# Left-side tiles moved by 192 bytes, and tokens' high and low part moved in one 512-column product over stationary weights

## Chip, core and metric

The kernel runs on one core of one Trainium2 chip. The metric is the device time of one execution in microseconds (us), the median of several runs. TensorE multiplies, VectorE and ScalarE move and transform tiles between SBUF and PSUM, GpSimd does a few small operations, and SyncE issues the DMAs that load weights.

## What is computed

A trunk of four post-norm layers over 256 tokens of width 1024. Each layer has a token mixer (layers 0 and 3 a gated linear recurrence, layer 1 an RWKV-7 time mix, layer 2 chunked attention), a cross-attention of 4 heads into 256 memory tokens, and an MLP with a squared ReLU. Cut to what matters:

```python
def memory_cross_attention(x, mem, w_q, w_kv, w_o):
    q = (x @ w_q).reshape(bsz, seq, MEM_HEADS, MEM_HEAD_DIM)
    kv = (mem @ w_kv).reshape(bsz, mem.shape[1], 2, MEM_HEADS, MEM_HEAD_DIM)
    s = jnp.einsum('bqhd,bkhd->bhqk', q, kv[:, :, 0]) * (MEM_HEAD_DIM ** -0.5)
    p = jax.nn.softmax(s, axis=-1)
    o = jnp.einsum('bhqk,bkhd->bqhd', p, kv[:, :, 1]).reshape(bsz, seq, d)
    return o @ w_o

def squared_relu_mlp(x, w1, w2):
    return jnp.square(jax.nn.relu(x @ w1)) @ w2

for i in range(DEPTH):
    y = mixer(i)(h)
    h = _layer_norm(DEEPNORM_ALPHA * h + y, ln_g[i, 0], ln_b[i, 0])
    y = memory_cross_attention(h, mem, mx_w_q[i], mx_w_kv[i], mx_w_o[i])
    h = _layer_norm(DEEPNORM_ALPHA * h + y, ln_g[i, 1], ln_b[i, 1])
    y = squared_relu_mlp(h, mlp_w1[i], mlp_w2[i])
    h = _layer_norm(DEEPNORM_ALPHA * h + y, ln_g[i, 2], ln_b[i, 2])
```

All inputs and weights are float32.

## The kernel before

**Three products for one.** Large matrix products are made in the type float32r from split operands. A float32 tile is split into a high part (ScalarE casts it to float32r, L436 and L338) and a low part (VectorE subtracts the high part, L437 and L339), and a product of two split operands is the sum of high × high, high × low and low × high. Each of the three is one matrix multiplication with a weight load of its own (the stationary operand) in front. Such three are called a trio below.

**Weights.** They come in chunks of 128 rows by 1024 columns (896 for the recurrence's input). A chunk is fetched by a DMA on SyncE's queue into wraw (four buffers) and split into whi and wlo (seven buffers each). A chunk is given back (`done`) when its last product is issued, and then the next chunk's split and DMA are issued; ScalarE and VectorE run their instructions in the order in which the code writes them.

**Two ways round.** `gemm` (and `mm_piece`, L272 to L274) has the tokens stationary, 128 by 128, and moves 512 (or 448) columns of weights. `gemm_t` has the weights stationary and moves the tokens, so that the result comes out transposed: four chunks, two halves m, in each half two output blocks g, and for every chunk two row blocks k; at each such place three products of 256 columns (L297, in `wt_steps`): whi × hthi, whi × htlo, wlo × hthi. The 256 columns are two runs of 128 tokens. `gemm_t` is used by the MLP's w1 for seven of its eight blocks (two banks of mm for m = 0, two of tp for m = 1; the first of the seven uses four banks of acc), for the second half of the cross-attention's q, and for three of the attention's six projections. It gives back the left 256 columns of each PSUM bank; the eviction is ScalarE's Relu (L709), a scaled copy (L960), or a cast and VectorE's subtraction (L610, L611). The memory pieces (`mem_piece`) run either `wt_steps` on the memory's tokens memhi and memlo, or trios of 512 columns with them stationary (L498).

**The MLP's loop.** For each block of 512 hidden columns: w1 of this block, then w2 of the block before (trios of 512 columns with ahi, alo stationary, 48 products). One round is 96 products of `gemm_t` and 48 of w2.

**Where tiles lie.** Pools are stacks in each partition's memory: the constants, LayerNorm's weights, the tokens (hthi, htlo) and every stage's own pool grow from the left, the weights (wraw, whi, wlo) and the memory's tiles from the right. The constant mhalf is 16 floats (64 bytes) and is the second tile of the left.

Of the kernel before, what the change touches and what calls it, by code (L numbers as in the profile page):

```python
# [7 lines left out]
F32 = mybir.dt.float32  # L8
F32R = mybir.dt.float32r
AF = mybir.ActivationFunctionType  # L10
ALU = mybir.AluOpType
# [5 lines left out]
T = 256  # L17
# [185 lines left out]
class _LazyT:  # L203
# [11 lines left out]

    def both(self, kt):

        return [x[:, :, kt, :] for x in self.hl]

    def __getitem__(self, t):  # L220
        if self.t[t] is None:
# [10 lines left out]
class Kern:  # L232
# [45 lines left out]
                self.st.done(c)  # L278

    def wt_piece(self, accs, chunks, both, m, last=False):  # L280
        for _ in self.wt_steps(accs, chunks, both, m, last):
            pass

    def wt_steps(self, accs, chunks, both, m, last=False):

# [28 lines left out]
    def gemm_t(self, name, idx, x, banks):  # L314

        ch = self.chunks(name, idx, 4, 128, 1024)
        for m in range(2):
            accs = [banks[m](), banks[m]()]
            self.wt_piece(accs, ch, x.both, m, last=m == 1)
            for g in range(2):  # L320
                yield 2 * m + g, accs[g][:, :T]

    def gemm(self, name, idx, nchunk, lhs, p, w, kpc=2):

# [62 lines left out]
            )  # L387

    def ht_pair(self, dt):
        return [self.ht_p.tile([128, 2, 8, 128], dt, name=n, tag=n) for n in ("hthi", "htlo")]  # L390

    def to_hl(self, src, hi, lo, n, o0=0):
        for i in range(0, n, 4):
# [128 lines left out]
    def cross(self, l, left):  # L522

        nc, tc = self.nc, self.tc
        with tc.tile_pool(name="cr", bufs=1, reuse_waits="tile") as p:
# [79 lines left out]
                self.side = side  # L605
            for t, a in self.gemm("w_q", (l, 0), 4, self.hT, 128, 512):
                nc.scalar.activation(qn[:, t, :], a, AF.Copy, scale=1.0 / 16)
            for c, a in self.gemm_t("w_q", (l, 1), self.hT, (self.acc, self.acc)):
                hi, lo = (x[:, c, :] for x in q[1])
                nc.scalar.activation(hi, a, AF.Copy, scale=1.0 / 16)  # L610
                nc.vector.scalar_tensor_tensor(out=lo, in0=a, scalar=1.0 / 16, in1=hi.bitcast(F32), op0=ALU.mult, op1=ALU.subtract)  # L611
                if c == 1:
                    scores(0, 0)
                    scores(1, 0)
# [77 lines left out]
    def mlp(self, l):  # L692
        nc, tc = self.nc, self.tc
        NB = 8
        with tc.tile_pool(name="mlp", bufs=2, reuse_waits="tile") as p:
            accs = None
            sq, aT = [], {}

            def w1(b):
                hi = p.tile([128, 4, T], F32R, name="ahi", tag="ahi")  # L700
                lo = p.tile([128, 4, T], F32R, name="alo", tag="alo")
                ts = [slice(t * 128, (t + 1) * 128) for t in range(2)]
                for t in range(2):
                    aT[b, t] = _hl(hi[:, :, ts[t]], lo[:, :, ts[t]])
                if b:
                    for c, a in self.gemm_t("w1", (l, b), self.hT, (self.acc, self.acc) if b == 1 else (self.mm, self.tp)):
                        if c % 2 == 0:
                            r = p.tile([128, 2, T], F32, name="rel", tag="rel")
                        nc.scalar.activation(r[:, c % 2, :], a, AF.Relu)  # L709
                        if c % 2:  # L710
                            sl = slice(c - 1, c + 1)
                            nc.vector.tensor_tensor(out=r, in0=r, in1=r, op=ALU.mult)  # L712
                            nc.scalar.copy(hi[:, sl, :], r)
                            nc.vector.tensor_tensor(out=lo[:, sl, :], in0=r, in1=hi[:, sl, :].bitcast(F32), op=ALU.subtract)
                            while sq:
                                self.to_hl(*sq.pop(0), 4)
                    return
                ch = self.chunks("w1", (l, b), 4, 128, 1024)
                for t in range(2):
                    a = self.mm()  # L720
                    self.mm_piece(a, ch, self.hT[t], 128, 512, last=t == 1, near=None if t else lambda: self.hT[1])
                    r = p.tile([128, 512], F32, name="rel", tag="rel")
                    nc.scalar.activation(r, a, AF.Relu)
                    nc.vector.tensor_tensor(out=r, in0=r, in1=r, op=ALU.mult)
                    sq.append((r, hi[:, :, ts[t]], lo[:, :, ts[t]]))

            for b in range(NB + 1):
                if b < NB:
                    w1(b)
                if b == 0:  # L730
                    continue
                if b == 1:
                    accs = [[self.acc() for _ in range(2)] for _ in range(2)]
                chs = [self.chunks("w2", (l, b - 1, nh), 2, 128, 1024) for nh in range(2)]
                near = self.next_ht() if b == NB else None
                for t in range(2):
                    for nh in range(2):
                        self.mm_piece(accs[t][nh], chs[nh], aT[b - 1, t], 128, 512, start=b == 1, stop=b == NB,
                                      last=t == 1 and b < NB, near=near if t and nh else None)
                        if b == NB:  # L740
                            if t == 0 and nh == 0:
                                self.st.more()
                            self.resid(t, nh, accs[t][nh])
                    if b == NB:
                        self.ln_end(t, chs[0] + chs[1])
                if b == 5 and self.coming("rwkv"):
                    self.rw_first()
# [202 lines left out]
    def attn(self, l, j):  # L950
        nc, tc = self.nc, self.tc
        with tc.tile_pool(name="at", bufs=1, reuse_waits="tile") as p:
# [3 lines left out]

            def piece(i):
                if 0 < i < 4:
                    for c, a in self.gemm_t("ca_qkv", (j, i), self.hT, (self.acc, self.acc)):
                        nc.scalar.activation(qkT[i // 2][:, 4 * (i % 2) + c, :], a, AF.Copy, scale=0.125 if i < 2 else 1.0)  # L960
                    return
                for t, a in self.gemm("ca_qkv", (j, i), 4, self.hT, 128, 512):
                    if i >= 4:
                        nc.scalar.copy(vn[t][:, (i - 4) * 512:(i - 3) * 512], a)
                    else:
                        s = p.tile([128, 512], F32, name="an", tag="an", bufs=2)
                        nc.scalar.activation(s, a, AF.Copy, scale=0.125)
                        nat.append(s)
# [142 lines left out]
    def rwkv(self, l, j):  # L1111
# [4 lines left out]
        r1, r2 = ExitStack(), ExitStack()  # L1116
        R1 = r1.enter_context(tc.tile_pool(name="rwa", bufs=1, reuse_waits="tile"))
        R2 = r2.enter_context(tc.tile_pool(name="rwb", bufs=1, reuse_waits="tile"))
        rc = R2.tile([128, RC_P], F32, name="rc")
        nc.sync.dma_start(rc, self.I["rw_const"][:, :RC_P])  # L1120
        cumM, cumX, w3 = rc[:, 0:128], rc[:, 128:256], rc[:, 256:262]
        two = lambda P, n: [P.tile([128, D], F32, name=f"{n}{t}", tag=f"{n}{t}") for t in range(2)]
        r, k, a, s = two(R1, "r"), two(R2, "k"), two(R2, "a"), two(R2, "s")
# [1 line left out]
        tg = R1.tile([128, T], F32, name="tg")  # L1125
        bs = [R1.tile([128, 16], F32, name=f"bs{t}") for t in range(2)]
        rkrow = R2.tile([128, D], F32, name="rkrow", tag="rkrow")
        Dc = R2.tile([128, 3, 8], F32, name="Dc")
        state = [R2.tile([128, 4, 64], F32, name=f"st{f}") for f in range(2)]
        hv = lambda x: x.rearrange("p (a b) -> p a b", b=64)  # L1130
        bc = lambda x, p=128: x.unsqueeze(2).to_broadcast([p, 8, 64])
# [588 lines left out]
    def run(self):  # L1720
# [14 lines left out]
        with ExitStack() as ctx:  # L1735
# [12 lines left out]
            self.ident = self.c_p.tile([128, 128], F32, name="ident")  # L1748
            if not self.dry:
                make_identity(nc, self.ident[:, :])  # L1750
            self.mhalf = self.c_p.tile([128, 16], F32, name="mhalf")
            nc.vector.memset(self.mhalf, -0.5)
            self.hT = _LazyT(self)
            self.h = [self.c_p.tile([128, D], F32, name=f"h{t}") for t in range(2)]
# [161 lines left out]
```

## Time and profile before

| | |
|---|---|
| median of 3 runs | 1821.97 us (1815.96 to 1825.61) |
| the profiled execution's own time | 1830.35 us |
| its span, first to last instruction | 1828.6 us |
| TensorE busy | 1761.9 us, 96% |
| VectorE busy | 1201.0 us, 66% |
| ScalarE busy | 867.9 us, 47% |
| mean granted TensorE clock | 0.989 of full speed |

A row of the view by line is a group of equal instructions: line, engine, operation, output and inputs with partitions × elements, count, then the busy time, the mean ns of one, and the idle time before them. Consecutive products overlap in TensorE, so a mean is longer than the distance between two starts; distances are read from the start times of the timeline, or from the chain of work, which merges equal instructions that follow each other without a gap.

### The profile page before, as it was taken

How to read it: one execution, taken by the hardware profiler on the slowest of the kernel's cores; microseconds unless marked ns; L12 is line 12 of the kernel's file. 1: busy time of each engine (PE TensorE's matmuls, PEld its weight loads, DVE VectorE, ACT ScalarE, POOL GpSimd, SP SyncE). 2: the span in 40 equal slices, each digit the busy share in tenths (PEclk: the TensorE clock that was granted, in tenths of full speed). 3: DMA queues.
4: the chain of work that ended last, by engine and by line, in shares of the span. 5: the costliest groups of instructions: out<-in, count | busy, mean ns of one | idle time of the engine just before them, and what ended most of it. 6: DMA issues, size and time to landing. Idle time of an engine off the chain costs nothing.

```text
span 1828.6 us, 27714 instructions
## 1 busy us (share of the span) xinstructions
PE 1761.9 (96%) x11152; PEld 1511.1 (83%) x11152; DVE 1201.0 (66%) x1669; ACT 867.9 (47%) x1322; POOL 55.3 (3%) x64
## 2 busy tenths in 40 slices
PE   8979999999999889999999999999999999999998
PEld 7777989998677566888888888889998887989886
DVE  6477675567478698775556566865557587676555
ACT  6654545444444123544444553634444674545442
POOL 2000000000010001000000000000000000000000
PEclk9999999999999999999999999999999999999999
DMA  7455556555341323455555723545555545536552
GB/s 238 137 170 164 179 163 219 187 190 169 129 139 69 117 71 120 157 185 196 187 192 185 254 92 127 190 162 190 184 185 176 177 137 164 210 116 229 187 186 89
DMA packets 92933, 302.50 MB, mean 165 GB/s; under 512 B 11906, under 2 KB 19586, under 8 KB 92676
## 3 DMA queue, kind: packets, MB, share of 16 engines
q1 hardware_dynamic: 91780, 297.92, 49.8%
q10 hardware_dynamic: 1024, 2.81, 0.6%
q8 instruction: 87, 1.43, 0.3%
q14 instruction: 42, 0.34, 0.1%
HBM read 299.65 MB, written 1.05 MB: 164 GB/s over the span
## 4 chain that ended last, share of the span: by engine, by line
PE 78%; DVE 11%; DMA 4%; ACT 3%; issue 2%; POOL 0%; SPq 0%; DVEq 0%; ACTq 0%
PE acc L274 11%; PE acc L273 11%; PE acc L272 11%; PE acc L297 10%; PE tp L297 7%; PE mm L297 7%; PE acc L498 4%; DVE wlo L437 3%; PE acc L192 2%; PE mm L817 2%; PE tp L335 2%; DMA wraw<-in_lru_in 2%; PE mm L467 1%; ACT whi L436 1%; PE mm L587 1%
## 5 line engine op out<-in xcount | busy, mean ns | idle before, releaser
L437 DVE TENSOR_TENSOR wlo<-wraw,whi 128x1024 fp32r<-128x1024 f32 (+3 forms) x505 | 594.9, 1207 | 190.0 <-ACT whi L436 187.2
L436 ACT CAST whi<-wraw 128x1024 fp32r<-128x1024 f32 (+3 forms) x505 | 507.2, 1038 | 214.4 <-PE acc L274 142.1
L272 PE MATMUL acc<-whi,ahi 128*128 128x512 f32 x512 | 202.0, 395 | 0.0
L274 PE MATMUL acc<-whi,alo 128*128 128x512 f32 x512 | 201.8, 394 | 0.0
L273 PE MATMUL acc<-wlo,ahi 128*128 128x512 f32 x512 | 201.7, 394 | 0.0
L272 PE MATMUL acc<-whi,hthi 128*128 128x448 f32 (+1 forms) x368 | 143.3, 390 | 5.6 <-ACT whi L436 5.6
L273 PE MATMUL acc<-wlo,hthi 128*128 128x448 f32 (+1 forms) x368 | 141.7, 385 | 3.2 <-DVE wlo L437 3.2
L274 PE MATMUL acc<-whi,htlo 128*128 128x448 f32 (+1 forms) x368 | 141.3, 384 | 0.0
L712 DVE TENSOR_TENSOR rel<-rel 128x512 f32<-128x512 f32 x56 | 38.6, 689 | 135.5 <-ACT rel L709 135.5
L274 PEld LDWEIGHTS acc<-whi,alo 128*128 128x128 f32 x512 | 95.7, 187 | 23.7
L272 PEld LDWEIGHTS acc<-whi,ahi 128*128 128x128 f32 x512 | 95.8, 187 | 22.3
L273 PEld LDWEIGHTS acc<-wlo,ahi 128*128 128x128 f32 x512 | 95.8, 187 | 22.2
L297 PE MATMUL mm<-hthi,whi 128*128 128x256 f32 x384 | 107.6, 280 | 0.0
L297 PE MATMUL tp<-hthi,whi 128*128 128x256 f32 x384 | 107.5, 280 | 0.0
L297 PE MATMUL mm<-hthi,wlo 128*128 128x256 f32 x384 | 107.3, 279 | 0.0
L297 PE MATMUL mm<-htlo,whi 128*128 128x256 f32 x384 | 107.2, 279 | 0.0
L297 PE MATMUL tp<-htlo,whi 128*128 128x256 f32 x384 | 107.1, 279 | 0.0
L297 PE MATMUL tp<-hthi,wlo 128*128 128x256 f32 x384 | 107.1, 279 | 0.0
L297 PE MATMUL acc<-hthi,whi 128*128 128x256 f32 x352 | 99.3, 282 | 1.3 <-ACT qkT L960 1.3
L297 PE MATMUL acc<-hthi,wlo 128*128 128x256 f32 x352 | 98.2, 279 | 0.0
L297 PE MATMUL acc<-htlo,whi 128*128 128x256 f32 x352 | 98.1, 279 | 0.0
L338 ACT CAST hthi<-tp 128x512 fp32r<-128x512 f32 x40 | 22.8, 588 | 137.7 <-PE tp L335 136.7
(393 smaller groups left out, 3749.7 us busy)
## 6 DMA issues: line engine op xcount, KB each, us to landing
wraw<-in_w SPq DMA_DIRECT2D x256, 512.0 KB, 4.6
wraw<-in_w_kv SPq DMA_DIRECT2D x64, 512.0 KB, 4.6
wraw<-in_lru_in SPq DMA_DIRECT2D x47, 448.0 KB, 4.5
wraw<-in_w_q SPq DMA_DIRECT2D x32, 512.0 KB, 4.3
wraw<-in_w_co SPq DMA_DIRECT2D x32, 512.0 KB, 4.4
wraw<-in_ca_qkv SPq DMA_DIRECT2D x24, 512.0 KB, 5.2
wraw<-in_lru_out SPq DMA_DIRECT2D x24, 448.0 KB, 5.2
ln_gt<-in_ln_g SPq DMA_DIRECT2D x12, 512.0 KB, 6.5
```

What stands on the lines that cost most here:

```text
L192: return f(*a, **k)
L272: nc.tensor.matmul(acc[:, :w], lhsT=a, rhs=wh[:p, ws], start=s, stop=False)
L273: nc.tensor.matmul(acc[:, :w], lhsT=a, rhs=wl[:p, ws], start=False, stop=False)
L274: nc.tensor.matmul(acc[:, :w], lhsT=b, rhs=wh[:p, ws], start=False, stop=e)
L297: self.nc.tensor.matmul(a, lhsT=w[:, ws], rhs=v, start=s and i == 0, stop=e and i == 2)
L335: self.nc.tensor.transpose(dst_ps[:n, j * p:(j + 1) * p], s, self.ident[:p, :p])
L338: self.nc.scalar.copy(hi, ps)
L436: self.nc.scalar.copy(hi, src)
L437: self.nc.vector.tensor_tensor(out=lo, in0=src, in1=hi.bitcast(F32), op=ALU.subtract)
L498: nc.tensor.matmul(a, lhsT=u, rhs=w[:, ws], start=s, stop=e)
L712: nc.vector.tensor_tensor(out=r, in0=r, in1=r, op=ALU.mult)
L817: nc.tensor.matmul(ps[:CT, gate * T:(gate + 1) * T], lhsT=gw[gate][:, n, :], rhs=xc[g][:, k, :], start=n == ks[0][0], stop=n == ks[-1][0])
```

## The change

`gemm_t` makes two products where it made three. The tokens' high and low part now lie in one tile ht (four runs of 128 tokens per row block: high of both token halves, low of both), and whi is multiplied with all four runs at once, 512 columns into a whole PSUM bank; wlo is multiplied with the high runs into the left half. The bank then holds two parts that must be added: ScalarE copies the right half into SBUF, VectorE adds the left half to it. In the MLP the Relu moves into the square (a maximum with zero, times itself). In the cross-attention a tile qs takes the sum, in a place (tag ol0) that is free then. `wt_steps` stays as it was for the memory pieces.

The constant mhalf grows from 16 to 64 floats, so every later tile of the left side lies 192 bytes further. In the RWKV mix two tiles of odd size are padded (rc by 24 floats, Dc from 24 to 64), so that what follows them keeps its place modulo 128. In both programs these are the byte addresses modulo 128:

| tiles | side | before | after |
|---|---|---|---|
| wraw, whi, wlo, memhi, memlo | right | 96 | 96 |
| hthi, htlo (after: ht) | left | 32 | 96 |
| MLP's ahi, alo; cross-attention's P, ol | left | 32 | 96 |
| cross-attention's qh, ql, kh, kl, vh, vl | left | 32 | 96 |
| recurrence's yhi, ylo; RWKV's mxhi, mxlo | left | 32 | 96 |
| attention's oT | left | 32 | 96 |
| RWKV's oT (four tiles) | left | 64, 64, 64, 32 | 96 |

```diff
     def both(self, kt):
-        return [x[:, :, kt, :] for x in self.hl]
+        hi, _ = self.tiles()
+        return hi[:, :, kt, :], self.k.ht[:, :, kt, :]
...
     def wt_piece(self, accs, chunks, both, m, last=False):
-        for _ in self.wt_steps(accs, chunks, both, m, last):
-            pass
+        n = len(chunks)
+        for ci, c in enumerate(chunks):
+            if not self.dry:
+                wh, wl = self.st.hl[c]
+                for k in range(2):
+                    x, xy = both(2 * ci + k)
+                    s, e = ci + k == 0, ci == n - 1 and k == 1
+                    for g in range(2):
+                        ws = slice(k * 512 + (2 * m + g) * 128, k * 512 + (2 * m + g + 1) * 128)
+                        four = accs[g][:, :].rearrange("p (t n) -> p t n", t=4)
+                        self.nc.tensor.matmul(four, lhsT=wh[:, ws], rhs=xy, start=s, stop=False)
+                        self.nc.tensor.matmul(four[:, :2], lhsT=wl[:, ws], rhs=x, start=False, stop=e)
+            if self.side:
+                self.side()
+            if last:
+                self.st.done(c)
...
             for g in range(2):
-                yield 2 * m + g, accs[g][:, :T]
+                yield 2 * m + g, accs[g][:, :T], accs[g][:, T:]
...
     def ht_pair(self, dt):
-        return [self.ht_p.tile([128, 2, 8, 128], dt, name=n, tag=n) for n in ("hthi", "htlo")]
+        x = self.ht_p.tile([128, 4, 8, 128], dt, name="ht", tag="ht")
+        self.ht = x
+        return [x[:, 0:2], x[:, 2:4]]
...
-            for c, a in self.gemm_t("w_q", (l, 1), self.hT, (self.acc, self.acc)):
+            for c, a, a2 in self.gemm_t("w_q", (l, 1), self.hT, (self.acc, self.acc)):
                 hi, lo = (x[:, c, :] for x in q[1])
+                if c == 0:
+                    qs = p.tile([128, 4, T], F32, name="qs", tag="ol0")
+                nc.scalar.copy(qs[:, c, :], a2)
+                nc.vector.tensor_tensor(out=qs[:, c, :], in0=a, in1=qs[:, c, :], op=ALU.add)
+                a = qs[:, c, :]
...
-                        nc.scalar.activation(r[:, c % 2, :], a, AF.Relu)
+                        nc.scalar.copy(r[:, c % 2, :], a2)
+                        nc.vector.tensor_tensor(out=r[:, c % 2, :], in0=a, in1=r[:, c % 2, :], op=ALU.add)
                         if c % 2:
                             sl = slice(c - 1, c + 1)
-                            nc.vector.tensor_tensor(out=r, in0=r, in1=r, op=ALU.mult)
+                            nc.vector.scalar_tensor_tensor(out=r, in0=r, scalar=0.0, in1=r, op0=ALU.max, op1=ALU.mult)
...
-                        nc.scalar.activation(qkT[i // 2][:, 4 * (i % 2) + c, :], a, AF.Copy, scale=0.125 if i < 2 else 1.0)
+                        o, sc = qkT[i // 2][:, 4 * (i % 2) + c, :], 0.125 if i < 2 else 1.0
+                        nc.scalar.activation(o, a2, AF.Copy, scale=sc)
+                        nc.vector.scalar_tensor_tensor(out=o, in0=a, scalar=sc, in1=o, op0=ALU.mult, op1=ALU.add)
...
-        rc = R2.tile([128, RC_P], F32, name="rc")
-        nc.sync.dma_start(rc, self.I["rw_const"][:, :RC_P])
+        rc = R2.tile([128, RC_P + 24], F32, name="rc")
+        nc.sync.dma_start(rc[:, :RC_P], self.I["rw_const"][:, :RC_P])
...
-        Dc = R2.tile([128, 3, 8], F32, name="Dc")
+        Dc = R2.tile([128, 8, 8], F32, name="Dc")[:, :3]
...
-            self.mhalf = self.c_p.tile([128, 16], F32, name="mhalf")
+            self.mhalf = self.c_p.tile([128, 64], F32, name="mhalf")
```

How the instructions stand on the engines, at three places. First TensorE in an MLP, where w1's block begins after w2 of the block before (a row is line, operation, output and inputs, size; the numbers tell buffers apart). Before:

```order
L274 MATMUL acc_2571<-whi_2520,alo_2311 128x512
L297 MATMUL mm_2646<-hthi_2248,whi_2538 128x256
L297 MATMUL mm_2646<-htlo_2249,whi_2538 128x256
L297 MATMUL mm_2646<-hthi_2248,wlo_2539 128x256
L297 MATMUL mm_2647<-hthi_2248,whi_2538 128x256
L297 MATMUL mm_2647<-htlo_2249,whi_2538 128x256
L297 MATMUL mm_2647<-hthi_2248,wlo_2539 128x256
```

At the same place after:

```order
L275 MATMUL acc_2517<-whi_2472,alo_2285 128x512
L294 MATMUL mm_2592<-ht_2223,whi_2486 128x512
L295 MATMUL mm_2592<-ht_2223,wlo_2487 128x256
L294 MATMUL mm_2593<-ht_2223,whi_2486 128x512
L295 MATMUL mm_2593<-ht_2223,wlo_2487 128x256
```

Of the three products for each bank the first two became one of 512 columns, and the third stayed.

Second VectorE in layer 1's cross-attention, from the softmax of the first heads to that of the last; ql is the low part of q, nm the row maximum of the scores that need it. Before:

```order
L437 TENSOR_TENSOR vl<-vn_4763,vh 128x512
L611 SCALAR_TENSOR_TENSOR ql_6493<-acc,qh_6492 128x256 x2
L339 TENSOR_TENSOR ql_6780<-tp,qh_6779 128x512 x2
L563 TENSOR_REDUCE nm<-acc 128x2
L567 RECIPROCAL ssum<-ssum 128x2
```

After:

```order
L456 TENSOR_TENSOR vl<-vn_4540,vh 128x512
L632 TENSOR_TENSOR qs<-acc,qs 128x256
L635 SCALAR_TENSOR_TENSOR ql_6268<-qs,qh_6267 128x256
L632 TENSOR_TENSOR qs<-acc,qs 128x256
L635 SCALAR_TENSOR_TENSOR ql_6268<-qs,qh_6267 128x256
L356 TENSOR_TENSOR ql_6532<-tp,qh_6531 128x512 x2
L582 TENSOR_REDUCE nm<-acc 128x2
```

An addition came in front of each of the two subtractions; on ScalarE a copy came in front of each of the two casts.

Third VectorE in the attention's projections, from the split of the memory's tokens on. Before:

```order
L437 TENSOR_TENSOR wlo<-wraw,whi 128x1024 x5
L437 TENSOR_TENSOR memlo<-kT,memhi 128x1024 x2
L437 TENSOR_TENSOR wlo<-wraw,whi 128x1024 x4
L974 COPY qkT_8839<-tp 128x4x128 x2
L437 TENSOR_TENSOR wlo<-wraw,whi 128x1024 x16
```

After:

```order
L456 TENSOR_TENSOR wlo<-wraw,whi 128x1024 x5
L456 TENSOR_TENSOR memlo<-kT,memhi 128x1024 x2
L987 SCALAR_TENSOR_TENSOR qkT_8393<-acc,qkT_8393 128x256 x2
L456 TENSOR_TENSOR wlo<-wraw,whi 128x1024 x4
L987 SCALAR_TENSOR_TENSOR qkT_8393<-acc,qkT_8393 128x256 x2
L1001 COPY qkT_8393<-tp 128x4x128 x2
L987 SCALAR_TENSOR_TENSOR qkT_8394<-acc,qkT_8394 128x256 x2
L456 TENSOR_TENSOR wlo<-wraw,whi 128x1024 x4
```

VectorE's half of each eviction stands between the splits, where VectorE had no part in evictions.

## Rows read from the trace of the kernel before

**Rows 1.** The page: busy time, share of the span and instructions, by engine.

```profile
PE 1761.9 (96%) x11152; PEld 1511.1 (83%) x11152; DVE 1201.0 (66%) x1669; ACT 867.9 (47%) x1322; POOL 55.3 (3%) x64
```

**Rows 2.** Stretches: length, PE, PEld, DVE, ACT, POOL busy, clock, DMA share, GB/s.

```profile
16.00:134.00 118.00, 104.73 (x536) 92.93 (x535) 75.46 (x106) 75.05 (x124) 10.55 (x24) 0.94 0.56 165
...
283.00:443.00 160.00, 160.00 (x988) 142.44 (x988) 95.00 (x100) 73.38 (x98) 0.92 (x1) 1.00 0.57 189
```

**Rows 3.** By line and form, TensorE's products; count, busy us, mean ns, idle before.

```profile
L272 PE MATMUL acc<-whi,ahi 128*128 128x512 f32 x512 | 202.0, 395 | 0.0
...
L297 PE MATMUL mm<-hthi,whi 128*128 128x256 f32 x384 | 107.6, 280 | 0.0
L297 PE MATMUL tp<-hthi,whi 128*128 128x256 f32 x384 | 107.5, 280 | 0.0
...
L297 PE MATMUL acc<-hthi,whi 128*128 128x256 f32 x352 | 99.3, 282 | 1.3 <-ACT qkT L960 1.3
...
L272 PE MATMUL acc<-whi,hthi 128*128 128x448 f32 x192 | 72.3, 377 | 5.6 <-ACT whi L436 5.6
...
L272 PE MATMUL acc<-whi,hthi 128*128 128x512 f32 x176 | 71.0, 403 | 0.0
...
L272 PE MATMUL acc<-whi,P 128*128 128x512 f32 x128 | 50.8, 397 | 0.0
...
L272 PE MATMUL acc<-whi,yhi 112*128 112x512 f32 x96 | 38.2, 398 | 0.0
...
L272 PE MATMUL mm<-whi,hthi 128*128 128x512 f32 x64 | 25.6, 400 | 0.0
...
L272 PE MATMUL acc<-whi,mxhi 128*128 128x512 f32 x32 | 12.6, 395 | 0.0
```

**Rows 4.** The chain of work in layer 0's MLP: start us, us, what, count.

```profile
297.95 5.65 PE mm L297 x48
303.60 5.65 PE tp L297 x48
...
320.46 5.65 PE mm L297 x48
```

**Rows 5.** Timeline of TensorE in a memory piece: start us, us, what.

```profile
207.58 0.39 PE L498 MATMUL acc<-whi,memhi 128*128 128x512 f32 x1
...
211.66 0.39 PE L498 MATMUL acc<-whi,memhi 128*128 128x512 f32 x1
```

**Rows 6.** The chain in layer 0's cross-attention: q, memory pieces, scores.

```profile
188.53 5.45 PE acc L297 x48
...
194.85 11.51 PE acc L297 x96
...
217.72 2.87 PE acc L561 x24
```

**Rows 7.** Timeline of TensorE in the recurrence's input projection, 448 columns.

```profile
31.15 0.36 PE L272 MATMUL acc<-whi,hthi 128*128 128x448 f32 x1
...
35.40 0.36 PE L272 MATMUL acc<-whi,hthi 128*128 128x448 f32 x1
```

**Rows 8.** By line and form: evictions of 256 columns on ScalarE and VectorE.

```profile
L610 ACT ACTIVATE qh<-acc 128x256 fp32r<-128x256 f32 x16 | 5.9, 386 | 4.3 <-PE acc L297 4.3
L508 ACT COPY kT<-acc 128x256 f32<-128x256 f32 x16 | 5.6, 370 | 3.7 <-PE acc L297 3.6
...
L339 DVE TENSOR_TENSOR kl<-acc,kh 128x256 fp32r<-128x256 f32 x8 | 3.1, 420 | 3.5 <-ACT kh L338 3.5
```

**Rows 9.** Timeline in layer 1's cross-attention, from q's last products to the scores.

```profile
754.94 0.73 ACT L610 ACTIVATE qh<-acc 128x256 fp32r<-128x256 f32 x2 [1.26 <-PE acc L297]
...
755.36 0.78 DVE L611 SCALAR_TENSOR_TENSOR ql<-acc,qh 128x256 fp32r<-128x256 f32 x2 [0.65 <-ACT qh L610]
...
755.88 0.36 PE L561 MATMUL acc<-kh,qh 128*128 128x256 f32 x1
```

**Rows 10.** The attention's projections: VectorE's timeline, and the chain behind it.

```profile
1003.68 1.23 DVE L437 TENSOR_TENSOR memlo<-kT,memhi 128x1024 fp32r<-128x1024 f32 x1 [0.52 <-ACT memhi L436]
...
1003.98 22.88 PE acc L297 x192
```

More of the change, by code (lines that the diff above doesn't have):

```diff
@@ L705, in w1 @@
                 if b:
-                    for c, a in self.gemm_t("w1", (l, b), self.hT, (self.acc, self.acc) if b == 1 else (self.mm, self.tp)):
+                    for c, a, a2 in self.gemm_t("w1", (l, b), self.hT, (self.acc, self.acc) if b == 1 else (self.mm, self.tp)):
                         if c % 2 == 0:
                             r = p.tile([128, 2, T], F32, name="rel", tag="rel")
-                        nc.scalar.activation(r[:, c % 2, :], a, AF.Relu)
+                        nc.scalar.copy(r[:, c % 2, :], a2)
+                        nc.vector.tensor_tensor(out=r[:, c % 2, :], in0=a, in1=r[:, c % 2, :], op=ALU.add)
                         if c % 2:
                             sl = slice(c - 1, c + 1)
-                            nc.vector.tensor_tensor(out=r, in0=r, in1=r, op=ALU.mult)
+                            nc.vector.scalar_tensor_tensor(out=r, in0=r, scalar=0.0, in1=r, op0=ALU.max, op1=ALU.mult)
                             nc.scalar.copy(hi[:, sl, :], r)
@@ L958, in piece @@
                 if 0 < i < 4:
-                    for c, a in self.gemm_t("ca_qkv", (j, i), self.hT, (self.acc, self.acc)):
-                        nc.scalar.activation(qkT[i // 2][:, 4 * (i % 2) + c, :], a, AF.Copy, scale=0.125 if i < 2 else 1.0)
+                    for c, a, a2 in self.gemm_t("ca_qkv", (j, i), self.hT, (self.acc, self.acc)):
+                        o, sc = qkT[i // 2][:, 4 * (i % 2) + c, :], 0.125 if i < 2 else 1.0
+                        nc.scalar.activation(o, a2, AF.Copy, scale=sc)
+                        nc.vector.scalar_tensor_tensor(out=o, in0=a, scalar=sc, in1=o, op0=ALU.mult, op1=ALU.add)
                     return
```

## The prediction

> **What bounds the kernel now.** I read the page first: TensorE is busy 1761.9 of 1828.6 us, VectorE 66% of it [rows 1]. A share over the whole span hides stages, so the view by stretch came next. In the MLP of layer 0 TensorE is busy 160.00 of 160.00 us at the full granted clock, while VectorE has 95.00 and ScalarE 73.38; in the recurrent stage of layer 0 it is busy 104.73 of 118.00, so there something else ends part of the time [rows 2]. The first to the last product of a stage thus cost what TensorE's issue costs, nearly everywhere. Then the trap in the view by line: it gives a 256-column product 280 ns and a 512-column one 395 ns [rows 3], which reads as if a product had a fixed cost of 165 ns, and as if two products in place of three would save a third. These durations overlap. What counts is the distance from start to start, and the chain of work has it: in the MLP 48 products of 256 columns take 5.65 us (117.7 ns each), the next 48 start at once, and the following round starts at 320.46, 22.51 us after this one; less the two times 5.65 that leaves 11.21 us for 48 products of 512 columns, 233.5 ns each [rows 4]. At 2.4 GHz the columns alone are 106.7 and 213.3 ns. So a product has 11 ns on top at 256 and 20 ns at 512, and three of 256 (353 ns) cost as much as one of 512 and one of 256 (351 ns).
>
> **Fewer products, same columns.** gemm_t is called 35 times, with 32 places each: 1120 places, which the three groups of L297 confirm (384 + 384 + 352) [rows 3]. At each, three products of 256 columns become one of 512 and one of 256. With the distances above: 233.5 + 117.7 − 353.1 = −1.9 ns, times 1120 = −2.1 us. By itself this part is next to nothing, and the evictions it adds (below) are as large.
>
> **The moved tiles.** What the 192 bytes do must be read from operands that already lie as the moved ones will. The front's table gives their places: before, a left-side operand lies at 32 (some at 64) modulo 128 bytes and the weight halves at 96; after, all lie at 96. Where do both operands of a product agree today? In the memory pieces, where memhi and memlo lie at 96 beside weights at 96. There, from 207.58 to 211.66 us, 18 products of 512 columns take 4.08 us: 226.7 ns, not 233.5, at the same clock and with a weight load each [rows 5]. At 256 columns the agreeing pairs are memhi with whi (96 products in 11.51 us, 119.9 ns) and the scores' kh with qh, both at 32 (24 in 2.87, 119.6 ns) [rows 6]. So agreeing operands have 13.3 ns on top of the columns whether these are 256 or 512, and differing ones 11 at 256, 20 at 512, and at 448, where 21 products take 4.25 us (202.4 ns), 15.7 [rows 7]. It is the agreement and not the side: kh and qh, both on the left, cost at 256 columns what memhi and whi, both on the right, do. At 512 columns only the right side shows an agreeing pair. That differing operands at 256 are not settled by the place alone is seen in one stretch of 48 at 5.45 us, 113.5 ns [rows 6].
>
> The price, with 680 ns for an agreeing trio of 512 columns (3 × 226.7) against 700:
> - Trios of 512 columns with a left-side stationary operand: 512 + 176 + 64 + 128 + 96 + 32 = 1008 [rows 3], each 20 ns: −20.2 us. (Two groups of oT, 64 trios, are left out: their place is 64 before, and 1.3 us more would be all.)
> - Trios of 448 columns: 192 [rows 3], 607 to 3 × (186.7 + 13.3) = 600 ns: −1.3 us.
> - gemm_t: the new pair at agreeing places is 226.7 + 119.9 = 346.6 ns against 353.1: −6.5 ns × 1120 = −7.3 us. The 512-column product there reads four runs of 128 columns, which no row shows; the 256-column products in two runs (memhi) cost as the one-run ones (kh), so I take 226.7. Its bounds: 240 (twice the two-run price, pair 360, +7.7 us) and 220 (6.8 ns on top, as in the 5.45 us stretch, with 113.5 for its partner: pair 333.5, −22.0 us).
>
> Together −28.8 us on TensorE. Of that the 448-column trios and the 96 of yhi (1.9 us) lie in the recurrent stage, where TensorE isn't always the bound [rows 2]; I strike half of their 3.2 us: +1.6.
>
> The pages of the Trainium skill speak against this part. "TensorE: Matmul & The Clock Gate", step-by-step of Part 2, says that the moving operand and the weight load have separate SBUF read ports and that loading the next weights takes nothing from the running product; its back-to-back gap is columns over 2.4 GHz plus 2.5 ns. By that no address could matter, the trio would be 327.5 ns, the pair 325 and the change worth −2.8 us of TensorE. The trace disagrees: 226.7 and 233.5 ns stand where that page of the Trainium skill has 215.8 [rows 4, 5].
>
> **What the two-part eviction adds.** ScalarE copies the low half where it applied the Relu or the scale (370 ns against 386 for such tiles [rows 8]), so no time there but for 16 new copies in the cross-attention. VectorE gets 140 additions of 256 columns (112 in the MLPs, 16 for q, 12 for the attention's q and k) at 420 ns [rows 8]: 58.8 us; the square becomes a max-and-multiply of the same tile. In an MLP it is 28 × 0.42 = 11.8 us on 95.00 of 160 [rows 2]; it hides, since mm's and tp's two banks come round only after a w2 part of 11.21 us [rows 4]. Where four acc banks go straight on to w2 (the first gemm_t of an MLP), the second pair's banks are wanted 24 products, 5.6 us, later; the eviction (a split's cast and subtraction ahead of it, then two additions) takes about 3.2. Hidden. If VectorE lost that slack, each pair would cost TensorE up to 0.8 us.
>
> Two places have no cover. In layers 1 and 2 nothing stands between the last gemm_t pair of q and the scores but 8 transposes. ScalarE starts at 754.94, VectorE's two subtractions follow at 755.36, the scores start at 755.88 [rows 9]: no wait. After the change, copy, addition, cast and subtraction run for one column block and then for the other, on two engines: 754.94 + 2 × (0.37 + 0.42 + 0.39) plus the last subtraction 0.42 and some 0.3 of hand-overs is 758.0, while the scores want the last block at 755.88 + 9 × 0.12 = 757.0. TensorE waits 1.0 to 1.2 us. Behind the eviction on both engines stands the split of the transposed probabilities, which pv(0) wants only after 24 score products more (2.9 us), so the wait is not paid twice: +2.4 for two layers. In layers 0 and 3 the memory pieces stand in between. In the attention's projections TensorE waits 1.3 us for ScalarE's eviction already; VectorE's half of it will queue behind a subtraction that ends at 1003.68 + 1.23 = 4.91, so the bank comes free at 1005.35 instead of 1003.98: +1.4 [rows 3, 10]. Four weight splits queue behind it, 0.84 us late, for chunks wanted a whole gemm_t (11.3 us) later. Bounds of these waits: 0 (transfers bind beside them) to 7 us (each twice). Taken: +3.8.
>
> **Sum.** −28.8 + 1.6 + 3.8 = −23.4 us against the profiled execution's 1830.35. That execution is 8.4 us over the median of 1821.97, and the cost per product is the same in every execution, so the forecast is 1821.97 − 23.4 = 1798.6, say 1799 us.
>
> **The rivals.**
> - *The four-run product is dear* (240 ns): the trios gain, gemm_t gives 7.7 back in place of 7.3: −23.4 + 15.0 = −8.4 us, 1814. For it: runs of 128 columns start off a boundary each. Against it: two runs cost nothing extra. 12%.
> - *Place does not matter*, and the memory pieces are quick for another reason (the stretch of 113.5 ns shows that a stretch can run quicker with no change of place). Then −2.1 + 3.8 = +1.7 us, 1824. The page of the Trainium skill named above would give this result too. Against it: 680 in memory pieces of three layers, 700 in every MLP. 13%.
> - *Slower:* place does not matter and the four-run product takes 240: 240 + 117.7 − 353.1 = +4.6 ns × 1120 = +5.2, with the waits at 7, +12.2 us, 1834. It decides, above the 0.5%, once the pair is over 358 ns (353.1 + (9.1 − 3.8) / 1.12 ns) and the trios stay at 700. The rows speak against both halves. 8%.
> - *Quicker still:* pair at 333.5 and no waits: −23.4 − 14.7 − 3.8, 1780. 4%.
>
> The forecast's own case has 63%, from 1791 (no wait, nothing struck) to 1805 (waits at 7, all of the recurrent stage's gain lost). The range takes in the first rival wholly and the lower half of the second (spread some 4 us by the waits) and leaves out the third and the last, about 19%: 1784 to 1823. Over 0.5% (9.1 us, about what a measurement here can tell from no change) faster: 63 + 4 + half of the first rival, 73%; within: 19%; slower: 8%.
>
> **What would show it.** In the profile after: an MLP round of 22.51 us becomes 32 × 0.3466 + 48 × 0.2267 = 21.97; TensorE's w2 trios start every 0.68 us; gemm_t pairs every 0.347 (0.360: first rival; 0.351 with trios at 0.70: second). A new wait of about 1 us of the scores for the subtraction stands in layers 1 and 2, and the attention's 1.3 us grows to 2.7. I am wrong if w2 still takes 11.2 us, or if VectorE's additions show up as what TensorE waits for inside an MLP.

## The result

The changed kernel takes 1813.4 us (median of 20 runs, 1802.4 to 1820.4) where the kernel before takes 1823.55 us (20 runs). The ratio is 0.9944, 95% interval 0.9932 to 0.9956: 10.2 us, or 0.56%, faster. The time lies inside the stated range and moved the forecast way; 23.4 us were forecast. The mean granted clock over the executions is the same, 0.991, for both kernels (20 executions of the changed one; 17 of the one before, from the runs beside the first experiments).

### The profile page after: what moved, and what is told of

It is laid out like the page before. It is cut to its first block, busy times and chain, and to the rows that moved or that the text cites. A ratio compares the mean times of both kernels' runs of the same rounds, so it can differ in the third digit from the quotient of the medians.

```text
span 1800.6 us, 25667 instructions
## 1 busy us (share of the span) xinstructions
PE 1736.4 (96%) x10032; PEld 1453.8 (81%) x10032; DVE 1252.3 (70%) x1809; ACT 871.6 (48%) x1338; POOL 55.3 (3%) x64
## 4 chain that ended last, share of the span: by engine, by line
PE 78%; DVE 11%; ACT 4%; DMA 4%; issue 2%; POOL 0%; SPq 0%; DVEq 0%; ACTq 0%
PE acc L275 12%; PE acc L273 12%; PE acc L274 12%; PE tp L294 5%; PE mm L294 5%; PE acc L314 4%; PE acc L294 4%; PE acc L517 4%; PE tp L295 3%; PE mm L295 3%; DVE wlo L456 2%; PE acc L192 2%; PE mm L842 2%; PE tp L352 2%; PE acc L295 2%
## 5 line engine op out<-in xcount | busy, mean ns | idle before, releaser
L273 PE MATMUL acc<-whi,ht 128*128 128x448 f32 (+1 forms) x368 | 142.4, 387 | 5.5 <-ACT whi L455 5.5
L274 PE MATMUL acc<-wlo,ht 128*128 128x448 f32 (+1 forms) x368 | 140.6, 382 | 3.5 <-DVE wlo L456 3.5
L275 PE MATMUL acc<-whi,ht 128*128 128x448 f32 (+1 forms) x368 | 140.4, 381 | 0.0
L294 PE MATMUL tp<-ht,whi 128*128 128x512 f32 x384 | 136.7, 398 | 0.0
L294 PE MATMUL mm<-ht,whi 128*128 128x512 f32 x384 | 136.5, 398 | 0.0
L294 PE MATMUL acc<-ht,whi 128*128 128x512 f32 x352 | 126.0, 400 | 1.9 <-DVE qkT L987 1.9
L273 PEld LDWEIGHTS acc<-whi,ahi 128*128 128x128 f32 x512 | 96.1, 188 | 20.2
L295 PE MATMUL tp<-ht,wlo 128*128 128x256 f32 x384 | 107.9, 281 | 0.0
L295 PE MATMUL mm<-ht,wlo 128*128 128x256 f32 x384 | 107.8, 281 | 0.0
L295 PE MATMUL acc<-ht,wlo 128*128 128x256 f32 x352 | 98.7, 280 | 0.0
L294 PEld LDWEIGHTS tp<-ht,whi 128*128 128x128 f32 x384 | 72.2, 188 | 18.0
L294 PEld LDWEIGHTS mm<-ht,whi 128*128 128x128 f32 x384 | 72.1, 188 | 17.6
```

The costliest lines, as they stand in the source:

```text
L273: nc.tensor.matmul(acc[:, :w], lhsT=a, rhs=wh[:p, ws], start=s, stop=False)
L274: nc.tensor.matmul(acc[:, :w], lhsT=a, rhs=wl[:p, ws], start=False, stop=False)
L275: nc.tensor.matmul(acc[:, :w], lhsT=b, rhs=wh[:p, ws], start=False, stop=e)
L294: self.nc.tensor.matmul(four, lhsT=wh[:, ws], rhs=xy, start=s, stop=False)
L295: self.nc.tensor.matmul(four[:, :2], lhsT=wl[:, ws], rhs=x, start=False, stop=e)
```

## The profile after

The page's row of busy time, which answers to [rows 1]: 1120 fewer products on TensorE, 140 more instructions on VectorE and 16 more on ScalarE.

```profile
PE 1736.4 (96%) x10032; PEld 1453.8 (81%) x10032; DVE 1252.3 (70%) x1809; ACT 871.6 (48%) x1338; POOL 55.3 (3%) x64
```

TensorE's timeline in the MLP of layer 0, for [rows 4]: the first product of a round, of its second half of gemm_t, of the first five trios of its w2 part, and of the next round.

```profile
284.55 0.39 PE L294 MATMUL mm<-ht,whi 128*128 128x512 f32 x1
...
290.19 0.40 PE L294 MATMUL tp<-ht,whi 128*128 128x512 f32 x1
...
295.84 0.40 PE L273 MATMUL acc<-whi,ahi 128*128 128x512 f32 x1
...
296.55 0.40 PE L273 MATMUL acc<-whi,ahi 128*128 128x512 f32 x1
...
297.24 0.40 PE L273 MATMUL acc<-whi,ahi 128*128 128x512 f32 x1
...
297.94 0.39 PE L273 MATMUL acc<-whi,ahi 128*128 128x512 f32 x1
...
298.62 0.39 PE L273 MATMUL acc<-whi,ahi 128*128 128x512 f32 x1
...
306.79 0.39 PE L294 MATMUL mm<-ht,whi 128*128 128x512 f32 x1
```

The round is 22.24 us, between the 22.51 of before and the 21.97 of the forecast. Its w2 part is 10.95 us against 11.21, 684 ns a trio (680 forecast): the first three trios are 0.71, 0.69 and 0.70 us apart, and only from the fourth on are they 0.68. Its gemm_t is 11.29 us against 11.30: 353 ns a pair, what three products took, where 346.6 was forecast.

One stretch of that MLP by engine (length, PE, PEld, DVE, ACT, POOL busy, clock, DMA share, GB/s), for the second of [rows 2], and VectorE's additions by line and form:

```profile
270.00:430.00 160.00, 160.00 (x801) 135.16 (x801) 106.60 (x129) 75.19 (x102) 0.92 (x1) 1.00 0.55 189
```

```profile
L734 DVE TENSOR_TENSOR rel<-mm,rel 128x256 f32<-128x256 f32 x48 | 18.6, 425 | 110.4 <-ACT rel L733 110.4
```

TensorE is busy all the time with VectorE 11.6 us busier: 425 ns an addition, hidden as forecast. Where nothing hides it, layer 1's queries (ScalarE, VectorE, TensorE), for [rows 9]:

```profile
734.32 0.37 ACT L631 COPY qs<-acc 128x256 f32<-128x256 f32 x1 [0.36 <-PE acc L295]
...
734.90 0.41 DVE L632 TENSOR_TENSOR qs<-acc,qs 128x256 f32<-128x256 f32 x1
...
735.67 0.35 ACT L631 COPY qs<-acc 128x256 f32<-128x256 f32 x1
...
737.04 0.42 DVE L635 SCALAR_TENSOR_TENSOR ql<-qs,qh 128x256 fp32r<-128x256 f32 x1 [0.48 <-ACT qh L634]
...
737.07 0.39 PE L580 MATMUL acc<-kh,qh 128*128 128x256 f32 x1 [0.40 <-ACT qh L634]
```

The chain of copy, addition, cast and subtraction runs for one column block and then for the other, and ends 3.1 us after it began (3.06 forecast); the scores wait. TensorE's waits, summed over the span (what for, us, times, longest):

```profile
PE acc L294 <- DVE qkT L987: 1.9, 1, 1.9
PE acc L580 <- ACT qh L634: 1.7, 3, 0.9
...
PE mm L352 <- DVE P L588: 0.9, 1, 0.9
```

Before, the attention's wait was 1.3 [rows 3], the scores' none, and that for the probabilities 0.2: about 3.0 us of new waits.

## The experiments

**Two halves of the change.** First the 512-column product and its eviction alone, the tiles where they were.

```diff
-self.mhalf = self.c_p.tile([128, 64], F32, name="mhalf")
+self.mhalf = self.c_p.tile([128, 16], F32, name="mhalf")
...
-Dc = R2.tile([128, 8, 8], F32, name="Dc")[:, :3]
+Dc = R2.tile([128, 3, 8], F32, name="Dc")
```

> The changed kernel with the tiles left where they were before (left-side operands at 32 modulo 128 bytes, weights at 96): the product of 512 columns and the two-part eviction alone. Theory (the places made the gain): trios stay at 700 ns, the pair costs 347 to 353, the waits of layers 1 and 2 are there: 0 to +6 us against before, 1823 to 1830. Rival (the product over high and low part made the gain, the places nothing): 10 us under before, 1813.

Measured: 1827.1 us against 1824.4 of before, ratio 1.0024 (1.0012 to 1.0037): slower by 2.7 us by the medians, by 4.4 by the ratio. TensorE's timeline of one MLP round and of the next round up to its w2 part:

```profile
288.94 0.40 PE L294 MATMUL mm<-ht,whi 128*128 128x512 f32 x1
...
300.11 0.39 PE L273 MATMUL acc<-whi,ahi 128*128 128x512 f32 x1
...
311.31 0.39 PE L294 MATMUL mm<-ht,whi 128*128 128x512 f32 x1
...
322.60 0.41 PE L273 MATMUL acc<-whi,ahi 128*128 128x512 f32 x1
```

In the first round gemm_t takes 11.17 us (349 ns a pair), in the next 11.29 (353), and the rounds go on in turn like this; w2 takes 11.20, as before. So this half gains next to nothing on TensorE, and its waits cost more than that. It is not where the gain comes from.

Then the places alone, with gemm_t in three products.

```diff
-self.mhalf = self.c_p.tile([128, 16], F32, name="mhalf")
+self.mhalf = self.c_p.tile([128, 64], F32, name="mhalf")
...
-rc = R2.tile([128, RC_P], F32, name="rc")
+rc = R2.tile([128, RC_P + 24], F32, name="rc")
...
-Dc = R2.tile([128, 3, 8], F32, name="Dc")
+Dc = R2.tile([128, 8, 8], F32, name="Dc")[:, :3]
```

> The kernel before with the 192 bytes and the two padded tiles alone, gemm_t still in three products of 256 columns. Theory: trios of 512 columns fall from 700 to 680 ns (1008 of them, 20 us) and gemm_t's trio rises from 353 to the 360 that the memory pieces and scores show (1120 of them, 8 us), no new waits: 12 to 14 us under before, about 1810, as quick as the full change or a little quicker. Rival (the places are worth nothing, or another resource gives it back): within 3 us of before.

Measured: 1813.6 us, ratio 0.9942 (0.9928 to 0.9957), as quick as the whole change: some 10.6 us under before, where 12 to 14 were expected. The chain of work in layer 0's MLP (start, us, what, count):

```profile
291.07 5.75 PE mm L297 x48
296.82 5.76 PE tp L297 x48
...
313.49 5.75 PE mm L297 x48
```

gemm_t takes 11.51 us (360 ns a trio, up from 353) and w2 10.91 (682 ns, down from 700), both as expected within 2 ns. The places make the whole gain; that they cost gemm_t 7 ns a place is what the new pair then takes back, and pays for with its waits.

**The pair in the MLPs alone**, so that no wait has lost its cover:

```diff
-for c, a, a2 in self.gemm_t("w_q", (l, 1), self.hT, (self.acc, self.acc)):
+for c, a, _ in self.gemm_t("w_q", (l, 1), self.hT, (self.acc, self.acc), trio=True):
...
-for c, a, a2 in self.gemm_t("ca_qkv", (j, i), self.hT, (self.acc, self.acc)):
+for c, a, _ in self.gemm_t("ca_qkv", (j, i), self.hT, (self.acc, self.acc), trio=True):
```

> The changed kernel, but the queries and the attention's projections keep gemm_t's three products and the eviction in one part; only the MLPs have the pair. Theory (the waits of the scores in layers 1 and 2 and of the attention cost some 5 us in the changed kernel, and half-clock stretches that follow them a little more): 3 to 6 us under the changed kernel's 1813, less 2 us for 224 trios of 360 in place of pairs of 352: 1808 to 1812. Rival (these waits cost nothing, the missing half lies in the MLPs): 1813 to 1816.

Measured: 1813.1 us, ratio 0.9938 (0.9924 to 0.9951), by the ratios 1 us under the changed kernel. The scores' wait for the queries is gone from the list of waits and that for the probabilities is back at 0.2. The trios in q and the attention cost some 1.8 us more, so the waits are worth about 3; but a difference of 1 us with intervals of this width cannot bear that by itself. Inconclusive.

**The price of a place, by itself.** Equal products on resident tiles, nothing beside them; `o`, in floats of 4 bytes, moves the moving operand:

```python
for o in range(0, 512, 8):
    for i in range(REP):                      # REP = 12
        mm(ps[:, :512], lhsT=w, rhs=x[:, o:o + 512], start=i == 0, stop=i == REP - 1)
```

> No part of the network is computed: one resident pair of tiles, rows of 12 equal fp32r products each, first 512 columns in one run with the moving operand's place raised in steps of 32 bytes over 2048, then 256 columns in one run over 1024 bytes, then 256 columns in two runs 4096 bytes apart and 512 columns in four runs, both in steps of 64 bytes over 4096. Nothing else runs beside them. Theory (the two operands' places set the time): 512 columns at 226.7 ns where the places agree modulo 128 or 256 and 233.5 elsewhere; four runs between 227 and 241 by the place in steps of 512 bytes. Rival (contention with other engines' traffic makes the difference): one time for all places of a form, at or under 227.

TensorE in windows from the first product of one case to the first of the next, 12 products each (length, busy; the count has a product or two still running from the case before). The first five are 512 columns in one run, the moving operand 0, 32, 64, 96 and 192 bytes above the weights; then 256 columns in one run at 0, 256 in two runs at 0 and at 192, and 512 in four runs at 0, 64 and 192:

```profile
50.86:53.58 2.72, 2.72 (x14) 1.00 0.02 6
53.58:56.38 2.80, 2.80 (x13) 1.00 0.00 0
56.38:59.14 2.76, 2.76 (x14) 1.00 0.00 0
59.14:61.95 2.81, 2.81 (x14) 1.00 0.00 0
67.55:70.34 2.79, 2.79 (x13) 1.00 0.00 0
229.09:230.52 1.43, 1.43 (x14) 1.00 0.00 0
274.50:275.93 1.43, 1.43 (x15) 1.00 0.00 0
278.77:280.15 1.38, 1.38 (x14) 1.00 0.00 0
364.86:367.59 2.73, 2.73 (x14) 1.00 0.02 6
367.59:370.35 2.76, 2.76 (x13) 1.00 0.00 0
373.15:375.94 2.79, 2.79 (x13) 1.00 0.00 0
```

512 columns cost 227 ns at a difference of 0, 230 at 64 and 232 to 234 elsewhere, and the list repeats every 256 bytes. 256 columns are quickest (115 ns) with two runs at 192. Four runs at 0 cost 228, nearly like one: the 226.7 taken for the pair's first product was right for that product by itself. The rival, contention with other engines, falls: nothing else ran. This map moves only the moving operand. In w2 it is the stationary one that moves, and there too the trio follows the difference: 700 ns at 192, 682 at 0 (e2) and 687 at 64 (e6, below). In the programs the weights lie at 224 modulo 256, the left-side tiles at 32 before, 224 after and 160 in e6.

**The price of a sequence.** gemm_t's 32 places on resident tiles, the six forms that the expectation names at eight places each.

```python
def alternate(mm, accs, wh, wl, x, o, m, view):
    for kt in range(8):
        for g in range(2):
            mm(four(accs[g], 4), lhsT=wh[kt // 2][:, ws(kt % 2, m, g)], rhs=view(x, o, kt, 4), ...)
            mm(four(accs[g], 2), lhsT=wl[kt // 2][:, ws(kt % 2, m, g)], rhs=view(x, o, kt, 2), ...)
```

> No part of the network is computed: gemm_t's 32 places on resident tiles laid out as in the kernel (weight halves of four chunks, a moving tile with four runs), eight places of the moving tile from 0 to 224 bytes modulo 256 beside the weights, nothing running beside. Six forms: the pair as in the change; the same products with the two of 512 columns of a place ahead of its two of 256; four and four by chunk; the three products of 256; and the first and third with high and low part side by side in one run. Theory A (alternating two sizes costs what the products by themselves do not: 227.9 + 118.8 = 346.7 ns in the map of single products against the 350 to 361 of the changed kernel): the pair at place 0 takes 350 to 355 here too, grouped four and four it comes down to 347 to 348, the trio takes 358 to 360. Theory B (other engines' reads of the SBUF lengthen it in the full kernel): 347 for every order at place 0.

Windows as above, each of 32 places: the pair in turn at a difference of 0 and of 32; grouped by two at 0; by four at 0; three products of 256 at 0, at 64 and at 192; and the pair in turn at 0 with high and low part in one run:

```profile
58.10:69.41 11.31, 11.31 (x67) 1.00 0.00 0
69.41:80.51 11.10, 11.10 (x67) 1.00 0.01 1
147.92:159.06 11.14, 11.14 (x66) 1.00 0.00 0
...
237.21:248.42 11.21, 11.21 (x66) 1.00 0.00 0
326.82:338.34 11.52, 11.52 (x99) 1.00 0.01 1
349.65:360.96 11.31, 11.31 (x99) 1.00 0.01 1
395.12:406.03 10.91, 10.91 (x98) 1.00 0.01 2
417.39:428.49 11.10, 11.10 (x67) 1.00 0.00 0
```

The pair as in the change takes 353 ns a place with nothing beside it, the full kernel's figure; by two it takes 348, by four 350 (347 to 348 expected). But alternating sizes isn't dear everywhere: at a difference of 32 the same pair takes 347, less than the 352 that its two products (one run each) add up to in the map. The trio takes 360 at a difference of 0 and 353 at 64, the figures of e2 and of the kernel before, and 341 at 192; the kernel before has that price in one place, the second half of q, at 64 [rows 6]. With one run in place of four the pair takes 347. The next runs took these figures into the full kernel.

**Another order of the pair**, the two products of 512 columns of a place first:

```diff
-for g in range(2):
-    ...
-    self.nc.tensor.matmul(four, lhsT=wh[:, ws], rhs=xy, start=s, stop=False)
-    self.nc.tensor.matmul(four[:, :2], lhsT=wl[:, ws], rhs=x, start=False, stop=e)
+for g in range(2):
+    self.nc.tensor.matmul(four[g], lhsT=wh[:, ws[g]], rhs=xy, start=s, stop=False)
+for g in range(2):
+    self.nc.tensor.matmul(four[g][:, :2], lhsT=wl[:, ws[g]], rhs=x, start=False, stop=e)
```

> The changed kernel with the four products of one place of gemm_t in another order: the two of 512 columns first, then the two of 256. Theory (alternating sizes at agreeing places costs 353 ns where the grouped order costs 348 in the pair map): 5 to 6 us under the changed kernel. Rival (the pair's price in the kernel comes from contention): within 2 us of it.

The chain of work, from the first pair of a half gemm_t to that of the next half:

```profile
293.08 0.45 PE mm L294 x2
...
298.65 0.46 PE tp L294 x2
```

5.57 us for 16 places, 348 ns, as in the map. The time is 1810.4 us, ratio 0.9931 (0.9913 to 0.9948). The changed kernel itself, on the same chip, is the next one.

> The changed kernel itself, beside the two others on the same chip: 0.994 of before by every theory; it is there to compare them with, and to have its clock beside theirs.

It came to 1812.3 us, ratio 0.9944 (0.9926 to 0.9962). The new order's price is shown in the trace; its 2 us in the time, where 5 to 6 were expected, lie within the intervals.

**High and low part side by side**, one run in place of four:

```diff
-x = self.ht_p.tile([128, 4, 8, 128], dt, name="ht", tag="ht")
-self.ht = x
+x = self.ht_p.tile([128, 8, 4, 128], dt, name="ht", tag="ht")
+self.ht = x = x.rearrange("p k t n -> p t k n")
```

> The changed kernel with the high and low part of a place side by side in the token tile, so that the 512-column product reads one run of 2048 bytes (and its partner one run of 1024) in place of four and two; places, order and evictions as in the change. Theory (what costs the 6 ns is the four-run product in alternation with the two-run one at agreeing places; the pair map has 346.8 ns for one run and 353.4 for four): the pair 347 ns, 28 MLP rounds 0.2 us shorter, 6 to 7 us under the changed kernel's 1813. Rival (alternation of the two sizes alone, whatever the runs): the pair stays at 353, within 2 us of the changed kernel.

The theory falls. Timeline of an MLP round:

```profile
291.71 0.39 PE L294 MATMUL mm<-ht,whi 128*128 128x512 f32 x1
297.35 0.40 PE L294 MATMUL tp<-ht,whi 128*128 128x512 f32 x1
303.00 0.40 PE L273 MATMUL acc<-whi,ahi 128*128 128x512 f32 x1
313.94 0.39 PE L294 MATMUL mm<-ht,whi 128*128 128x512 f32 x1
```

11.29 us for gemm_t, as with four runs, and 1812.9 us, ratio 0.9939 (0.9920 to 0.9959). So in the kernel the number of runs is not what costs; why one run was quicker in the map, after other work, stays open.

**The place that the map points to**, with three products and no new eviction: the left-side tiles moved by 128 bytes, so that the moving tokens lie 192 above their weights, and moving weights 64 above their tokens.

```diff
-self.mhalf = self.c_p.tile([128, 64], F32, name="mhalf")
+self.mhalf = self.c_p.tile([128, 48], F32, name="mhalf")
```

> The kernel before with the left-side tiles moved by 128 bytes instead of 192 (and the same two pads), gemm_t in three products, so that a moving left operand lies 192 modulo 256 above its weights, and moving weights 64 above their left operand. Theory (the maps of products alone hold in the kernel): gemm_t's trio 341 ns against 353 of before (1120 times, 14 us), the 512-column trios 687 against 700 (1008 times, 13 us), no new waits: 24 to 28 us under before, 1797 to 1800. Rival (only agreeing places are quick, the other values of the map are lost among the kernel's other work): trios at 700, gemm_t at 353, within 5 us of before.

Measured: 1804.3 us, ratio 0.9889 (0.9868 to 0.9910): 20 us under the kernel before and some 10 under the changed one, the quickest of all. The chain of work:

```profile
296.16 5.47 PE mm L297 x48
301.62 5.44 PE tp L297 x48
...
318.05 5.47 PE mm L297 x48
```

gemm_t 10.91 us (341 ns a trio), w2 10.99 (687): the map's figures to the nanosecond. An MLP round is 21.89 us, 0.62 under before, and the four MLPs give some 16 of the 20 us. Part of what is missing from the 24 to 28 expected is where the same places don't give the map's price: the cross-attention's output trios stay at 700 ns in layers 0, 2 and 3 (687 in layer 1), the recurrence's output trios at 700 in layer 0 (687 in layer 3), and the second half of q takes 354 where it took 340 before. Why is not shown.

**A second profile of the kernel before**, unchanged:

> The kernel before itself, for a second profile of it: the first one was the longest of all its executions, and stage differences against the changed kernel taken from it may be its own. Theory: products as in the first profile (353 and 700 ns), the span near its median, and a stage-by-stage difference to the changed kernel's second profile of 10 to 14 us, of it 12 in the MLPs, less 4 to 5 in the scores. Rival (the lost gain lies in a stage where TensorE is not the bound): the MLPs give 12 and another stage gives back more than the waits of the scores.

Measured: 1824.2 us, ratio 0.9998 (0.9975 to 1.0020). The first product of the recurrent stage's output projection in layer 0, in the two profiles of before:

```profile
130.24 0.47 PE L272 MATMUL acc<-whi,yhi 112*128 112x512 f32 x1
```

```profile
126.05 0.48 PE L272 MATMUL acc<-whi,yhi 112*128 112x512 f32 x1
```

and in the two of the changed kernel:

```profile
118.92 0.47 PE L273 MATMUL acc<-whi,yhi 112*128 112x512 f32 x1
```

```profile
127.73 0.48 PE L273 MATMUL acc<-whi,yhi 112*128 112x512 f32 x1
```

Up to this point two executions of one program differ by 4 and by 9 us, more than the change can be worth there. The pair of profiles that the work began with (spans 1828.6 and 1800.6) differs by 28 us, and 11.3 of it stand at this marker. From the marker to the end it is 1698.4 and 1698.1 us before, 1681.7 and 1686.2 after: 12 to 17 us of gain. By the start times of the same products in the second pair, each MLP gives 2.2 us, 9 in all where 12 were expected, and the scores and probabilities of layers 1 and 2 take back 4. So neither side is right: TensorE's first product to its last is 10.1 us shorter, as the theory had it, but the MLPs give less than both took them to.

## Why the forecast was right, and where not

- *TensorE's issue bounds the MLPs.* Right: 160.00 of 160.00 us busy before and after, and each nanosecond off a product came out of the round (e1, e2, e6).
- *The gain is in the places, not in the product count.* Right, by e1 (3 to 4 us slower) against e2 (10.6 faster). The w2 trio went from 700 to 684 ns, 682 in e2, where 680 was forecast. The rule behind it, agreement modulo 128, was too coarse: a difference of 128 costs 233 in the map, and the list repeats every 256. It gave the right answer here, since the change makes the places equal modulo 256.
- *gemm_t's pair at 346.6 ns.* Wrong, and the largest miss. The 226.7 and 119.9 were each right for products in a row of their own kind (227 and 119 in e3), and their sum was taken to hold when they alternate. It doesn't, at these places: 353 in the kernel and, with nothing beside it, in e5. That is 6.4 ns on 1120 places, 7.2 of the 7.3 us forecast for this term. The first rival had nearly this time (1814) and the wrong reason: four runs by themselves cost nothing (e3), nor do they in the kernel's pair (e10); 5 of the 6.4 ns go when the order changes (e7). Why this order costs them is open.
- *VectorE's additions are hidden in the MLPs.* Right: 425 ns each, and no wait of TensorE for them.
- *New waits of 3.8 us.* Near: 3.0 by the list of waits, some 4 by the stages. The chain took 3.1 us for a forecast of 3.06, and the attention's wait grew by 0.6 where 1.4 was expected. What I had ruled out, that the delay is paid again behind the scores, shows as 0.7 us at the probabilities.
- *680 ns for all 1008 trios.* Wrong in size, the second miss. Most trios do take 680, but not all: in a round's w2 part the first four take 708, 692, 695 and 684 on average (701 and 700 before). Reckoned from start to start in the second pair of profiles (e9, e8), the 1008 trios give 14.7 us where 20.2 were forecast: w2 8.6 of 10.2, the 176 with tokens stationary 1.8 of 3.5, the other groups 4.3 of 6.4. The first pair has the same figures within 0.2.
- *The 448-column trios at 600 ns.* Wrong: 607 became 609 in one profile of after and 611 in the other (medians of 192). That agreeing operands have 13.3 ns on top at every width was taken from 256 and 512 columns and does not hold at 448; 600 came in e6, at a difference of 64. Half of this gain and of yhi's had been struck, 1.6 us, because TensorE isn't always the bound there. In the event yhi gave 1.6 of its 1.9 and the rest nothing, so what was struck is about right, by luck.
- *The sum.* In the second pair TensorE's first product to its last is 10.1 us shorter, and the terms add up to it: trios −14.7, gemm_t 0.0 with the attention's wait in it, the RWKV and attention oT −0.6 (left out of the forecast), scores and probabilities +4.0, all other products +1.2. The last is put down to scatter: it is −17 in the first pair, whose named terms are the same, and the two profiles of before differ by 4.7 us between themselves. With their waits the 448-column trios, counted in it, are −1.4 in one pair and +1.3 in the other. The runs say −10.2 (−8.0 to −12.4). So of the 13 us that were missing the pair accounts for 7.2 and the trios for 5.5.
- *The bounds of the forecast's own case.* By its own terms they are 1793 (−28.8) and 1803 (−28.8 + 3.2 + 7), not 1791 and 1805. The measured time lies outside either; the stated range holds it because it was drawn to take in the first rival, whose reason was wrong.

The page "TensorE: Matmul & The Clock Gate" of the Trainium skill says, in the step-by-step of Part 2, that weight load and moving operand have separate read ports and that loading the next weights takes nothing from the running product. The prediction read from this that no address matters, and from the page's back-to-back gap worked out an estimate of 215.8 ns for 512 columns. In e3 the same product takes 226.7 or 234 ns by its place alone, with no other engine at work; for these fp32r products the measurement decides against that reading.

## What to carry to other kernels

Where TensorE's issue is the bound, measure the start-to-start distance of the very sequence that will run: neither the durations by line nor the sum of two distances taken from rows of equal products gave the price of two sizes in turn. Where operands lie in SBUF can be a free parameter worth as much as a rewrite; a program of a few hundred microseconds that steps one operand through 256 bytes finds it, and its figures held in the kernel for most products of one size, though not for all (e6). And a steady price holds only after the first products of a row: check how many products a row has before multiplying. Before a stage's gain is read from a pair of profiles, a second profile of the same kernel shows how much of it is the stage's own scatter.

## What the hardware showed that I had not expected

- The time of an fp32r product follows the difference of its two operands' places modulo 256 bytes: 512 columns 227 ns at 0, 230 at 64, up to 234 elsewhere; three products of 256 in gemm_t's order 360 at 0, 353 at 64 and 341 at 192 (e3, e5, e6). What suits one size does not suit the other. Place isn't all: the second half of q takes 340 a trio at 64 and 354 at 192 (before, e6), the other way round.
- Two sizes in turn settle into another rhythm than either alone: at agreeing places 353 ns for the pair in place of 346, with the order worth 5 ns (e5, e7); at a difference of 32, 347 in place of 352 (e5); and at 64, 349 and 353 in alternate rounds of one kernel (e1). What sets it is not known.
- The recurrent stage of layer 0 ends 4 to 9 us apart in two executions of one program.
